# Layer B of a two-layer encoder: three units of two head pairs by one level of Strassen's products, its normalisation applied to x, and a reordered first microsecond

## The chip, the core and the metric

The kernel runs on one core of a Trainium2 chip. The metric is the device time of one execution in microseconds (us). The profile's rows name PE (matrix products), PEld (its weight loads), DVE (vector engine), ACT (scalar engine), POOL (GpSimd) and SP, which issues most DMAs.

## What is computed

Two layers over 512 tokens of width 1024, one batch. Layer A mixes tokens by dilated window attention (three dilation groups), layer B by neighbourhood attention on an 8 x 64 grid. Both have 16 heads of 64 columns, which the kernel handles as 8 pairs (`hc` 0 to 7).

```python
hn = rms_norm(x, norm_gain[i])
proj = hn @ w_in
q, k, v, gate = jnp.split(proj, 4, axis=-1)      # layer B
q = rms_norm(q, q_gain) * HEAD_DIM ** -0.5
k = rms_norm(k, k_gain)
...
p = jax.nn.softmax(logits)
y = (p @ v) * jax.nn.silu(gate)
x = x + y @ w_out
```

In layer B a pair takes 384 columns of q, k and v and 128 gate columns; the depth of each product is 1024.

## The kernel before, in words

All values are float32. Every matrix product is made from three of the reduced type: an operand is rounded by ACT (`_h`), the remainder is taken by a subtraction on DVE or POOL (`_l`), and `mm3` (L330) issues h x h, h x l and l x h into one PSUM bank. The activations stand in `hn_h` and `hn_l` (k = 0 to 7 slices of 128 x 512), the weights stream through 8 raw buffers (`wraw`), are rounded to `wh` (6 buffers) and split to `wl` (5 buffers).

`Plan` (L180) lists the weight blocks ("jobs") in the order of use, each 384 or 512 columns wide, and decides when the load of each is issued (`lead`, L269: 4, 12 or 6 jobs ahead) and whether POOL or DVE takes the remainder (`pool`, L296). `mixed` (L217) is the plan of a Strassen unit: four blocks of weights, two of which are added in place by DMAs that POOL issues with an accumulate (`add`, L209), and one sum on DVE (`sum`, L203). Only layer A has such units before.

PE's order is written by hand. `run` (L1163) lets a main generator emit the projections and a side generator emit the attention in between, by a clock that counts PE's work (`clock`, `stamp`, `later_on`). The other engines' order is the scheduler's, except where `in_order` or `keep_in_program_order` holds it.

In layer A, `main_a` (L692) makes the k, v, q columns of a pair by seven half-size products: `product` (L360) multiplies 4 slices of depth for two token tiles, and its evacuations combine the results (`put_v`, `put_u`, `put12`, `put22`, `put21`). The mixed left operands are made once by `mix` (L531) from x already multiplied by its norm factors (`scale_x`, L518).

In layer B, `main_b` (L1259) projects each pair plainly: `project_qk` (L622) takes 8 slices of depth for four token tiles, ACT multiplies the result by the row's norm factor on the way out of PSUM, POOL squares q and k, and `project_t` (L401) makes the gate, which DVE multiplies by half the norm factor (`rs_half`). `side_b` (L1275) is the attention of a pair: transposes of q and k, `scores`, `softmax` (DVE minimum, ACT exponential, ACT scaling), then the turn of the probabilities: by DVE transposes and a round trip through DRAM (`turner`, L914) for pairs 0 to 5, by PE transposes (`turn_p`, L1351) for pairs 6 and 7, then `weigh` and `put_y`. `out_product` (L1197) is the output projection; it starts on the pairs that are done.

At the start, `load_x` brings x in four loads between the weights' loads, the gains come by two small loads of ACT's queue, nine products of ones run on PE while it waits, and `square_a` (L510) squares each slice of x on ACT with a running sum on POOL.

Of the kernel before, what the change touches and what calls it, by code (L numbers as in the profile page):

```python
# [22 lines left out]
P = 128  # L23
# [4 lines left out]
KT = 8  # L28
# [7 lines left out]
PB = 4  # L36

# [9 lines left out]
def tile_hybrid_encoder(  # L47
# [5 lines left out]
    norm_gain: bass.AP,  # L53
    head_gain: bass.AP,
# [80 lines left out]
    mix_h = big.tile([P, 4, 4, H], F32R, tag="yh", name="mix_h")  # L135
    mix_l = big.tile([P, 4, 4, H], F32R, tag="yl", name="mix_l")
# [19 lines left out]

    def cast(raw, n):
        h = wp.tile([P, 512], F32R, tag="wh", name="wh", bufs=6)[:, :n]
        act.copy(h, raw)
        return h, raw, n  # L160
# [19 lines left out]
    class Plan:  # L180
# [22 lines left out]
        def sum(self, at, dst, a, b, eng):  # L203

            for raw in (dst, a, b):
                raw.used(at)
            self.sums.setdefault(at, []).append(lambda: eng.tensor_add(home(dst), a.tile, b.tile))

        def add(self, at, dst, off):  # L209

            dst.used(at)
            src = lambda: w[:, off : off + dst.cols]
            self.sums.setdefault(at, []).append(
                lambda: pol.dma_start(dst.tile, src(), accum_op=ALU.add)
            )

        def mixed(self, hc):  # L217
            b, j = hc * A_HC, len(self.jobs)
            b11, b21, b12, b22 = ([self.raw(b + 2048 * n + 1024 * i) for i in range(2)] for n in range(4))
            gate = self.raw(b - A_HC + 1152 * KT)  # L220
            v = self.raw(b - A_HC + 1024 * KT)
            t2 = [self.raw(None) for _ in range(2)]
            late = hc == 1
            order = (b11, gate, b21, b11, t2, b22, b12, v, t2) if late else (b11, gate, b21, v, b11, t2, b22, b12, t2)
            for part in order:
                for raw in part if isinstance(part, list) else [part]:
                    self.use(raw, 128 if raw in (gate, v) else 512)
# [23 lines left out]
    for hc in range(1, NHC):  # L251
        plan.mixed(hc)
# [11 lines left out]
    for hc in range(NHC):  # L264
        plan.plain(B_IN + hc * B_HC, 384, KT)
        plan.plain(B_IN + hc * B_HC + 384 * KT, 128, KT)
    outs(B_OUT)

    def lead(raw):  # L269
        return 4 if raw.first < start_jobs else 12 if raw.first < mixed_jobs else 6  # L270
# [46 lines left out]
    stamp = {("qk", -1): 0, ("w", -1): 0}  # L317
    stamp |= {("yb", -i, "y"): 0 for i in (1, 2, 3)}
# [41 lines left out]
    def product(acc, stat, open_, evac, guard=None):  # L360
# [4 lines left out]
        for k in range(KH):  # L365
# [4 lines left out]
            for i in range(2):  # L370
                sh, sl = (t[:, P * i : P * i + P] for t in stat(k))
                mm3(acc[i], sh, sl, h, l, open_ and k == 0, k == KH - 1, skip_group_check=True)
                if k == KH - 1:
                    evac(i, acc[i])
                yield

    def project(stat_h, stat_l, n, evac, guard, need=None, after=None):
# [3 lines left out]
        for k0 in range(0, KT, both):  # L381
# [6 lines left out]
            ws = [next(wsteps) for _ in ks]  # L388
            for i in range(4):
# [7 lines left out]
            if after:  # L397
                yield "xn", k0
                after(k0)
# [26 lines left out]
    later = []  # L426

    def head_norm(raw, ss, ns, late):
# [10 lines left out]
        if late:  # L439
            later.append(lambda: [tc.keep_in_program_order(scale(i)) for i in range(4)])  # L440
            return
# [17 lines left out]
    ng = cp.tile([P, 2, KT], F32, name="ng")  # L459
# [13 lines left out]
    pq = wk.tile([P, 4096], F32, tag="pt", name="pt", bufs=1)  # L473
    x_all = pq.rearrange("p (k t) -> p k t", k=KT)

    def load_x(k0, k1):
        syn.dma_start(x_all[:, k0:k1, :], xt[:, k0:k1, :])
# [5 lines left out]
    act.dma_start(ng, norm_gain)  # L483
# [6 lines left out]
    for _ in range(9):  # L490
# [4 lines left out]
    hg = cp.tile([P, 8], F32, name="hg")  # L495
    act.dma_start(hg, head_gain)
# [13 lines left out]
    def square_a(k):  # L510
# [3 lines left out]
        act.activation(sq, x_all[:, k, :], AF.Square)  # L514
# [3 lines left out]
    def scale_x():  # L518

        pa = spread()  # L520
        for k in range(KT):
            xk = x_all[:, k, :]
            vec.scalar_tensor_tensor(xk, xk, ng[:, 0, k : k + 1], pa, op0=ALU.mult, op1=ALU.mult)
            stamp["xn", k] = 0
# [6 lines left out]
    def mix():  # L531

# [3 lines left out]
        a, b = t[:, 0], t[:, 1]  # L536

        def put(n, out, op, x, y, eng, wait=0):
            def split():
                with in_order():  # L540
                    eng.tensor_sub(mix_l[:, n], out, mix_h[:, n].bitcast(F32))
                stamp["mix", n] = 0
# [5 lines left out]

        yield "wait", ("first",), 500
# [53 lines left out]
    rk = wk.tile([P, 4096], F32, tag="rawk", name="rawk", bufs=1)  # L603
# [5 lines left out]
    def raw_b(hc, cols):  # L609
        if hc % 3 < 2:  # L610
            return part(hc % 3, cols)
        if "third" not in st:
            st["third"] = wk.tile([P, 2048], F32, tag="rawq", name="rawb", bufs=1)
        return st["third"][:, : 4 * cols].rearrange("p (i c) -> p i c", i=4)

    def raw_q():
        return wk.tile([P, 4, 512], F32, tag="rawq", name="rawq", bufs=1)
# [4 lines left out]
    def project_qk(n, ns, key, hc, guard, first=False, **kw):  # L622
# [3 lines left out]
        def evac(i, acc):  # L626
            if not box:
                box.append(raw_q() if key == "rawq" else part(0) if key == "rawk" else raw_b(hc, n))
# [19 lines left out]
    def normed(raw, ss, ns, key, hc):  # L648

        def go():  # L650
            with in_order() if hc == 0 and key != "raw" else nullcontext():
                head_norm(raw, ss, ns, key == "raw")
# [39 lines left out]
    def main_a(hc):  # L692
        if hc == 0:
            yield from project_qk(512, 8, "rawq", hc, None, first=True, need="na")
            yield from project_qk(512, 4, "rawk", hc, ("rs", "a"), after=renorm)
# [10 lines left out]
        mixed = lambda n: lambda k: (t[:, n, k, :] for t in (mix_h, mix_l))  # L706
# [36 lines left out]
        for n, acc, first, put in ((0, c, True, put_v), (1, b, True, put_u), (3, c, False, put12), (2, b, False, put22)):  # L743
            yield "mix", n
# [103 lines left out]
    def put_y(hc, o, last):  # L848
# [4 lines left out]
        h, l = st["y_h"][:, hc, :], st["y_l"][:, hc, :]  # L853
        for grid, line in ((mid_rc, mid_o), (edge_rc, edge_o)):
            vec.tensor_mul(grid(gt), grid(gt), line(o))
        act.copy(h, gt)
        (vec if last else pol).tensor_sub(l, gt, h.bitcast(F32))
        stamp["yb", hc, "y"] = 0

# [9 lines left out]
    def y_back(hcs, tag):  # L869
        t = wk.tile([P, 4 * S], F32, tag=tag, name="yr", bufs=1)  # L870
        y = t[:, : len(hcs) * S].rearrange("p (n s) -> p n s", n=len(hcs))
        syn.dma_start(y, y_d[:, hcs[0] : hcs[-1] + 1, :])
        return t, y
# [40 lines left out]
    class turner:  # L914
# [12 lines left out]
        def send(self, dst, wait, pace, key=None):  # L927
# [8 lines left out]
            def read(b):  # L936
# [3 lines left out]
                if key and not self.left:  # L940
# [6 lines left out]
    def attn_a(hc):  # L947
# [202 lines left out]
        st["tail"], back = y_back(range(2), "tr")  # L1150
# [391 lines left out]
```

## Time and profile before

| what | us |
|---|---|
| median of 3 runs (lowest to highest) | 837.17 (836.69 to 837.88) |
| the profiled execution | 836.45 |
| its span on the core | 834.7 |
| layer A's pairs, about | 83 to 540 |
| its output product, about | 540 to 578 |
| layer B's pairs, about | 578 to 791 |
| last weighting and output product, about | 803 to 835 |

Times inside a profile count from the start of the span. The lines of each view are quoted in the prediction.

### The profile page before, as it was taken

Reading aid. Unit: us, or ns where it says so; the run is one execution under the profiler, and the core shown is the slowest. Engines: PE = TensorE matmul, PEld = TensorE weight load, DVE = VectorE, ACT = ScalarE, POOL = GpSimd, SP = SyncE. Lnnn points to the kernel's source line nnn. Section 1 sums busy time; section 2 is a strip of 40 time slices with the busy share of each in tenths; the row PEclk is TensorE's granted clock in tenths of the full one; section 3 lists DMA queues with packets and bytes.
Section 4 is the critical chain, followed back from the end, with each engine's and each line's share of the span. In section 5 each row is a group of like instructions: output and inputs, shape, how many; then the busy total and the mean of one; then the engine's idle time right before and its main releaser. Section 6 shows DMA issues by size and latency. Waiting matters only on the chain.

```text
span 834.7 us, 18138 instructions
## 1 busy us (share of the span) xinstructions
PE 821.2 (98%) x6611; PEld 685.0 (82%) x6611; DVE 631.2 (76%) x1653; ACT 506.6 (61%) x1066; POOL 292.9 (35%) x259
## 2 busy tenths in 40 slices
PE   8999999999999999999999999999999999999998
PEld 6877878878877878878878877789998899989786
DVE  7899897897897787786787866657578777876742
ACT  7657766846846846846846837645366654666440
POOL 5032442553543543543443424312133222333201
PEclk9999999999999999999999999999999999999999
DMA  9426756576686775775776664283254466544212
GB/s 340 149 57 164 195 148 160 120 177 206 121 183 203 164 170 174 164 175 169 161 170 180 137 195 158 75 296 111 93 186 153 126 170 190 165 143 138 86 51 102
DMA packets 56169, 131.97 MB, mean 158 GB/s; under 512 B 7184, under 2 KB 24528, under 8 KB 55952
## 3 DMA queue, kind: packets, MB, share of 16 engines
q1 hardware_dynamic: 49456, 108.39, 41.7%
q0 software_dynamic: 6048, 22.02, 15.2%
q8 instruction: 52, 0.85, 0.4%
q10 hardware_dynamic: 576, 0.41, 0.2%
q14 instruction: 37, 0.30, 0.1%
HBM read 111.73 MB, written 11.72 MB: 148 GB/s over the span
## 4 chain that ended last, share of the span: by engine, by line
PE 87%; DVE 4%; ACT 4%; DMA 3%; issue 1%; SPq 0%; DVEq 0%; ACTq 0%
PE acc L324 72%; PE log L324 5%; PE o L324 5%; PE tp L328 4%; DVE wl L85 1%; DMA wraw<-in_w 1%; DMA yr<-y_d 1%; DVE rawq L85 1%; ACT wh L85 1%; DMA pt<-in_xt 1%; ACT p L85 0%; ACT rawk L85 0%; DVE ss L85 0%; DVE mixed L85 0%; ACT sq L85 0%
## 5 line engine op out<-in xcount | busy, mean ns | idle before, releaser
L85 POOL TENSOR_TENSOR wl<-wraw,wh 128x512 fp32r<-128x512 f32 (+1 forms) x153 | 199.2, 1303 | 401.1 <-PE acc L324 161.4
L85 ACT CAST wh<-wraw 128x512 fp32r<-128x512 f32 (+1 forms) x360 | 208.5, 593 | 180.6 <-PE acc L324 137.1
L85 DVE TENSOR_TENSOR wl<-wraw,wh 128x512 fp32r<-128x512 f32 (+1 forms) x207 | 161.5, 783 | 39.0 <-PE acc L324 22.6
L324 PE MATMUL acc<-wh,hn_h 128*128 128x384 f32 (+1 forms) x488 | 184.4, 378 | 1.2 <-DVE rawq L85 1.2
L324 PE MATMUL acc<-wl,hn_h 128*128 128x384 f32 (+1 forms) x488 | 176.9, 362 | 2.9 <-DVE wl L85 2.9
L324 PE MATMUL acc<-wh,hn_l 128*128 128x384 f32 (+1 forms) x488 | 176.6, 362 | 0.0
L85 ACT ACTIVATE p<-p,mn 128x256 f32<-128x256 f32 (+2 forms) x248 | 138.2, 583 | 23.2 <-DVE mn L85 23.2
L324 PEld LDWEIGHTS acc<-wh,hn_h 128*128 128x128 f32 x488 | 91.7, 188 | 17.0 <-issue 6.8
L324 PEld LDWEIGHTS acc<-wl,hn_h 128*128 128x128 f32 x488 | 91.8, 188 | 11.9 <-DVE wl L85 4.7
L324 PEld LDWEIGHTS acc<-wh,hn_l 128*128 128x128 f32 x488 | 91.6, 188 | 9.6
L324 PE MATMUL acc<-wh,mix_h 128*128 128x512 f32 x224 | 89.0, 397 | 0.0
L324 PE MATMUL acc<-wh,mix_l 128*128 128x512 f32 x224 | 87.4, 390 | 0.0
L324 PE MATMUL acc<-wl,mix_h 128*128 128x512 f32 x224 | 87.3, 390 | 0.0
L324 PE MATMUL acc<-hn_h,wh 128*128 128x512 f32 x192 | 78.2, 407 | 0.0
L324 PE MATMUL acc<-hn_h,wl 128*128 128x512 f32 x192 | 75.3, 392 | 0.0
L324 PE MATMUL acc<-hn_l,wh 128*128 128x512 f32 x192 | 74.9, 390 | 0.0
L85 DVE STREAM_TRANSPOSE pt<-p 128x512 f32<-128x512 f32 (+1 forms) x60 | 40.6, 687 | 23.6 <-ACT p L85 23.4
L324 PE MATMUL acc<-y_h,wh 128*128 128x512 f32 x128 | 51.7, 404 | 0.5 <-ACT gt L85 0.5
L85 DVE TENSOR_REDUCE ss<-sq 128x4 f32<-128x256 f32 (+1 forms) x96 | 45.7, 498 | 8.1 <-ACT sq L85 4.3
L324 PEld LDWEIGHTS acc<-wh,mix_h 128*128 128x128 f32 x224 | 42.0, 188 | 9.8 <-issue 1.6
L324 PE MATMUL acc<-y_h,wl 128*128 128x512 f32 x128 | 50.0, 391 | 0.0
L324 PE MATMUL acc<-y_l,wh 128*128 128x512 f32 x128 | 49.9, 390 | 0.0
(148 smaller groups left out, 1358.5 us busy)
## 6 DMA issues: line engine op xcount, KB each, us to landing
wraw<-in_w SPq DMA_DIRECT2D x95, 512.0 KB
wraw<-in_w POOLq DMA_DIRECT2D x42, 512.0 KB, 7.0
wraw<-in_w SPq DMA_DIRECT2D x38, 384.0 KB
pt<-pt SPq DMA_DIRECT2D x106, 64.0 KB
td<-tr SPq DMA_DIRECT2D x24, 224.0 KB
pt<-td SPq DMA_DIRECT2D x24, 224.0 KB
e<-l_d SPq DMA_DIRECT2D x32, 112.0 KB
e<-l_d SPq DMA_DIRECT2D x16, 128.0 KB
```

Source lines behind the costliest of these rows:

```text
L85: m = f(*args, **kw)
L324: nc.tensor.matmul(o, l, r, **kw)
L328: nc.tensor.transpose(o, i, ident)
```

## The change

One: layer B. Pairs 0 and 1 keep the plain projection, without their gates. Pairs 2 to 7 become three units of two pairs, `unit_b`, each with seven products of 4 slices, two token tiles and 384 columns; the gates of the two pairs of the unit before are made inside the unit, those of 6 and 7 after the last. While pair 1 is projected, `scale_x(1)` multiplies x by the norm factors, `renorm` rounds it again into `hn_h` and `hn_l`, and `mix_b` makes the mixed operands. In the units the evacuations combine like layer A's, and the squares are ACT's. The outputs of pairs 0 to 3 go to DRAM (`y_d`) and come back in one load of 1 MB while the last unit ends. Pairs 6 and 7 are turned on PE after the last unit.

Two: the start. The gains stand in front of x in one array and come with its first slice. The squares stand behind the rounding of the next weights. The first step of the first projection issues h x h for all four token tiles, then h x l, then l x h. Eight products of ones instead of nine.

Also: one buffer of 6144 columns holds what were `rawk`, `rawq` and `rawb`, and `lead` and `pool` have entries for the units.

```diff
+        m = act.copy(h, raw)
+        if len(rounded) <= KT:
+            rounded.append(m.ins)
...
+        with tc.issue_after(rounded[k + 1]):
+            act.activation(sq, x_all[:, k, :], AF.Square)
...
-    for _ in range(9):
+    for _ in range(8):
...
+            if need and not k0:
+                h, l = ws[0]
+                for n_, (s, m) in enumerate(((stat_h, h), (stat_h, l), (stat_l, h))):
+                    for i in range(4):
+                        matmul(acc[i][:, :n], s(0, i), m, start=n_ == 0, stop=False)
+                        yield
+                continue
...
+    for hc in range(2, NHC, 2):
+        plan.mixed(in_b(hc + 1), in_b(hc), 384, gate_w(hc - 2), gate_w(hc - 1))
...
-            pool[0] = [0, 1] if first < 16 else [1, 2] if at < mixed_jobs else [2, 5]
+            pool[0] = [0, 1] if first < 16 else [1, 2] if at < mixed_jobs else [3, 5] if units_at <= at < units_end else [2, 5]
...
+    def mix_b():
+
+        put, a, b, x11, x12, x21, x22 = mixer(1)
+        put(0, a, vec.tensor_sub, x21, x22, pol)
...
-    def main_b(hc):
-        yield from project_qk(384, 4, "raw", hc, ("qk", hc - 1) if hc else ("rs", "b"))
-        acc = []
-        yield from project_t(acc)
...
-        tc.keep_in_program_order(vec.tensor_mul(gt, acc[0], st["rs_half"]))
...
+    def unit_b(r):
+
+        l = r + 1
...
+        def put11(i, acc):
+            act.copy(left[:, i, :], acc)
+            squares(left[:, i, :256], sl, i, 4)
+
+        def put_v(i, acc):
+            vec.tensor_sub(right[:, 2 + i, :], acc, left[:, 2 + i, :])
...
+        def put22(i, acc):
+            t = right[:, 2 + i, :]
+            vec.tensor_sub(t, t, acc)
+            squares(t[:, :256], sr, 2 + i, 4)
...
+        part_of = partial(product, cols=384)
+        yield from part_of(a, hn(0, 0), True, keep, ("w", r - 4))
+        yield from gate_a(r - 2)
+        yield from part_of(a, hn(KH, 0), False, put11)
+        yield from gate_a(r - 1)
+        yield "mix", 1, 0
+        yield from part_of(c, mixed(0), True, put_v, ("w", r - 3))
+        for n, acc, first, put in ((1, b, True, put_u), (3, c, False, put12), (2, b, False, put22)):
+            yield "mix", 1, n
+            yield from part_of(acc, mixed(n), first, put)
+        normed(right, sr, 4, "raw", r)
...
+        yield from part_of(b, hn(KH, H), False, put21)
+        normed(left, sl, 4, "raw", l)
+
+    def main_b():
...
+        yield from project_qk(384, 4, "raw", 0, ("rs", "b"))
+        yield from project_qk(384, 4, "raw", 1, None, after=(1, renorm))
+        stamp["renormed",] = 0
+        for r in range(2, NHC, 2):
+            yield from unit_b(r)
+        for hc in range(NHC - 2, NHC):
+            yield from gate_a(hc)
...
+            if hc == NHC - 4:
+                yield "wait", ("yb", "back"), 0
+                back = y_back(range(NHC - 4), wk.tile([P, 2048], F32, tag="tr", name="yr", bufs=1))
+                later_on(1000, partial(y_put, hc))
+                for n in range(NHC - 4):
+                    later_on(8000 + 2000 * n, partial(y_put, n, back[:, n, :]))
+                yield from side_b(hc + 2)
```

Three places show how the instructions move.

ACT at the very start, before. `pt` is x, `ng` the gains, `ssq` and `sqx` are the squares, `wh` the rounded weights.

```order
L85 ACTIVATE hn_h_92<-pt_98,ng_96 128x512
L85 ACTIVATE ssq_169<-pt_98 128x512
L85 CAST wh_125<-wraw_114 128x512
L85 ACTIVATE hn_h_92<-pt_98,ng_96 128x512
L85 ACTIVATE sqx_179<-pt_98 128x512
L85 CAST wh_127<-wraw_114 128x512
L85 ACTIVATE hn_h_92<-pt_98,ng_96 128x512 x2
```

The same place after the change:

```order
L84 ACTIVATE hn_h_92<-pt_95 128x512
L84 CAST wh_120<-wraw_109 128x512
L84 ACTIVATE hn_h_92<-pt_95 128x512
L84 CAST wh_122<-wraw_109 128x512
L84 ACTIVATE ssq_162<-pt_95 128x512
L84 ACTIVATE hn_h_92<-pt_95 128x512 x2
```

The first two roundings of weights now stand ahead of all squares.

PE in the projection of a middle pair, before: one weight block (`wh_8624`, `wl_8632`) serves four token tiles, that is twelve products, of which the last six are these.

```order
L324 MATMUL acc_8765<-wh_8624,hn_h_92 128x384
L324 MATMUL acc_8765<-wl_8632,hn_h_92 128x384
L324 MATMUL acc_8765<-wh_8624,hn_l_93 128x384
...
L324 MATMUL acc_8766<-wh_8624,hn_h_92 128x384
L324 MATMUL acc_8766<-wl_8632,hn_h_92 128x384
L324 MATMUL acc_8766<-wh_8624,hn_l_93 128x384
```

After the change, at the end of a unit's last mixed product (operands `mix_`) and the start of its last plain one:

```order
L332 MATMUL acc_8738<-wh_8814,mix_h_7376 128x384
L332 MATMUL acc_8738<-wl_8830,mix_h_7376 128x384
L332 MATMUL acc_8738<-wh_8814,mix_l_7377 128x384
L332 MATMUL acc_8739<-wh_8814,mix_h_7376 128x384
L332 MATMUL acc_8739<-wl_8830,mix_h_7376 128x384
L332 MATMUL acc_8739<-wh_8814,mix_l_7377 128x384
L332 MATMUL acc_8738<-wh_8828,hn_h_92 128x384
L332 MATMUL acc_8738<-wl_8849,hn_h_92 128x384
L332 MATMUL acc_8738<-wh_8828,hn_l_93 128x384
```

A weight block now serves two token tiles, six products; and bank `acc_8738`, which `put22` has to read after the mixed product, is written again by the product right behind it.

DVE at that same point of the unit, after the change (`rawk_153` is the buffer in which the results are combined):

```order
L84 TENSOR_TENSOR wl_8891<-wraw_8508,wh_8876 128x384
L84 TENSOR_TENSOR rawk_153<-rawk_153,acc_8738 128x384
L84 TENSOR_TENSOR wl_8937<-wraw_8712,wh_8899 128x384
L84 TENSOR_TENSOR rawk_153<-rawk_153,acc_8739 128x384
L84 TENSOR_REDUCE ss_8275<-sq_8907 128x4
```

The two subtractions into `rawk_153` are `put22` for the unit's two token tiles; a weight remainder stands between them. In layer B DVE had no such combinations before.

More of the change, by code (lines that the diff above doesn't have):

```diff
@@ L36 @@
 PB = 4
+G = 24
 A_HC = 1280 * KT
@@ L213, in add, with mixed @@
             self.sums.setdefault(at, []).append(
-                lambda: pol.dma_start(dst.tile, src(), accum_op=ALU.add)
+                lambda: pol.dma_start(dst.tile[:, : dst.cols], src(), accum_op=ALU.add)
             )
[L217 to L223, printed above, removed]
+        def mixed(self, left, right, n, gate, v, late=False):
+            j, c = len(self.jobs), 2 * n
+            b11, b21, b12, b22 = ([self.raw(b + c * (k + i), c) for i in range(2)]
+                                  for b in (left, right) for k in (0, 2))
+            gate, v = self.raw(gate), self.raw(v)
+            t2 = [self.raw(None, c) for _ in range(2)]
             order = (b11, gate, b21, b11, t2, b22, b12, v, t2) if late else (b11, gate, b21, v, b11, t2, b22, b12, t2)
@@ L607, in part, with raw_b @@
         return half.rearrange("p (i c) -> p i c", i=4)
[L609 to L614, printed above, removed]
+    def raw_b(hc):
+        at = 1536 * (0, 1, 3, 2, 1, 0, 2, 3)[hc]
+        return rk[:, at : at + 1536].rearrange("p (i c) -> p i c", i=4)
     def raw_q():
-        return wk.tile([P, 4, 512], F32, tag="rawq", name="rawq", bufs=1)
+        return rk[:, 4096:].rearrange("p (i c) -> p i c", i=4)
     def sums():
@@ L1155, in attn_a @@
         yield from q_a(hc + 1)
-        _, more = y_back(range(2, NHC - 2), "rawq")
+        more = y_back(range(2, NHC - 2), rk[:, 4096:])
         for n in range(2, NHC - 2):
@@ L1273, in tile_hybrid_encoder @@
+    def main_b():
+        for key in ("gate", "pt", "w"):
+            for hc in range(NHC):
+                stamp.pop((key, hc), None)
+        yield from project_qk(384, 4, "raw", 0, ("rs", "b"))
[3 more added lines that the diff above has]
+            yield from unit_b(r)
+        for hc in range(NHC - 2, NHC):
+            yield from gate_a(hc)
     far = lambda hc: hc < NHC - 2
     def side_b(hc):
[L1276 to L1279 removed]
@@ L1359, in weigh @@
         def weigh():
-            assert not any(t.left for t in turners)
             o = bank("o")
@@ L1407, in main @@
             st["e", hc] = bias_b(hc)
-        for hc in range(NHC):
-            yield from main_b(hc)
+        yield from main_b()
         yield from out_product("yb", sink_b)
@@ L1423, in side @@
         stamp["rs", "a"] = 0
-        for _ in scale_x():
+        for _ in scale_x(0):
             pass
@@ L1441, in side @@
         stamp["rs", "b"] = 0
-        yield 5000
-        st["rs_half"] = wk.tile([P, 2, S], F32, tag="q12", name="rs_half", bufs=1)[:, 0]
-        act.mul(st["rs_half"], spread(), 0.5)
-        stamp["rs", "all"] = 0
-        for hc in range(NHC):
-            yield from side_b(hc)
+        yield 3000
+        for _ in scale_x(1):
+            pass
+        yield 2000
+        yield from mix_b()
+        for hc in range(0, NHC - 2, 2):
+            yield from side_b(hc)
+            yield from side_b(hc + 1)
+            yield from weigh_b(hc)
+            if hc == NHC - 4:
[5 more added lines that the diff above has]
+                yield from side_b(hc + 2)
+            yield from weigh_b(hc + 1)
+            if hc == NHC - 4:
+                y_put(hc + 1)
+        hc = NHC - 2
+        yield from st.pop(("turn", hc))()
+        yield from side_b(hc + 1)
+        put_y(hc, st.pop(("weigh", hc))(), False)
+        yield 1000
+        yield from st.pop(("turn", hc + 1))()
+        stamp["yb", "turned"] = 0
+        put_y(hc + 1, st.pop(("weigh", hc + 1))(), True)
+        yield
         yield from residual(xm_d)
```

190 lines of the change are left out of this document (109 added, 81 removed).

## The prediction

> **What bounds the kernel now.** I read the page first: busy shares, then the chain that ended last, then the granted clock.
>
> ```profile
> span 834.7 us, 18138 instructions
> PE 821.2 (98%) x6611; PEld 685.0 (82%) x6611; DVE 631.2 (76%) x1653; ACT 506.6 (61%) x1066; POOL 292.9 (35%) x259
> PEclk9999999999999999999999999999999999999999
> PE 87%; DVE 4%; ACT 4%; DMA 3%; issue 1%; SPq 0%; DVEq 0%; ACTq 0%
> ```
>
> PE is busy 98% of the span, at full clock, and is 87% of the chain. Such a busy time can hide slack between pipelined products, so I next look at the pace of products in layer B, by their starts.
>
> ```profile
> 616.13 0.33 PE L324 MATMUL acc<-wl,hn_h 128*128 128x384 f32 x1
> ...
> 622.03 0.34 PE L324 MATMUL acc<-wh,hn_l 128*128 128x384 f32 x1
> ```
>
> These are two of 35 consecutive products of 384 columns: 34 intervals in 5.90 us, 0.1735 us each, although each row shows 0.33 us. Nothing lies between them: in layer B's projections PE issues without pause. The last view of this part is the busy time by stage (columns: window; its length, then PE, PEld, DVE, ACT, POOL busy with counts; clock; DMA share; GB/s).
>
> ```profile
> 140.00:202.00 62.00, 61.81 (x590) 49.89 (x588) 50.66 (x125) 39.65 (x79) 27.38 (x22) 1.00 0.68 170
> 681.10:734.70 53.60, 53.60 (x355) 49.19 (x354) 40.14 (x131) 32.21 (x86) 16.07 (x18) 1.00 0.56 167
> 37.00:43.00 6.00, 6.00 (x28) 4.97 (x27) 6.00 (x11) 3.64 (x7) 1.30 (x1) 1.00 0.28 87
> ```
>
> The first is one Strassen unit of layer A, the second two pairs of layer B. Both are PE's, and layer A shows that seven products with their sums can be fed: DVE 82%, ACT 64%, POOL 44%. The third shows DVE full for 6 us with PE losing nothing, since weights are prepared some jobs ahead.
>
> **The change part by part.** The sum is made against the profiled execution, 836.45 us (834.7 of span and 1.75 around it); the median of the runs, 837.17, is 0.7 above it.
>
> *Products removed.* A plain pair takes 8 slices x 4 tiles x 3 = 96 products of 384 columns, two pairs 192. A unit takes 7 x 4 x 2 x 3 = 168. Three units save 72, at 0.1735 us: **-12.5 us**. The gates, scores, transposes and weightings are the same in number. This is on the path wherever PE is.
>
> The Trainium skill, "TensorE: Matmul & The Clock Gate", section "Wait — 56ns, not 53.3ns?", gives N divided by 2.4 GHz plus about 2.5 ns for a warm product, 162.5 ns for 384 columns. By it the saving would be 11.7 us; the trace's 173.5 ns differ, and the measurement decides.
>
> *The start.*
>
> ```profile
> 3.87 0.72 ACT L85 ACTIVATE hn_h<-pt,ng 128x512 fp32r<-128x512 f32 x1 [0.70 <-DMA ng<-in_norm_gain]
> 4.50 0.62 ACT L85 ACTIVATE ssq<-pt 128x512 f32<-128x512 f32 x1
> 5.09 0.62 ACT L85 CAST wh<-wraw 128x512 fp32r<-128x512 f32 x1
> 5.76 0.80 PE L324 MATMUL acc<-wh,hn_h 128*128 128x512 f32 x1
> 6.95 0.50 PE L324 MATMUL acc<-wl,hn_h 128*128 128x512 f32 x1 [0.39 <-DVE wl L85]
> 19.68 0.50 PE L324 MATMUL acc<-wl,hn_h 128*128 128x512 f32 x1 [1.03 <-DVE wl L85]
> 14.44 3.49 DVE L85 SCALAR_TENSOR_TENSOR hn_l<-pt,ng,hn_h 128x512 fp32r<-128x512 f32 x2
> 21.25 1.40 DVE L85 SCALAR_TENSOR_TENSOR hn_l<-pt,ng,hn_h 128x512 fp32r<-128x512 f32 x2
> 14.27 3.12 POOL L85 TENSOR_TENSOR ssq<-ssq,sqx 128x512 f32<-128x512 f32 x2 [0.30 <-ACT sqx L85]
> ```
>
> ACT waits 0.70 us for the gains and squares for 0.62 us before it rounds the first weights: without both, the first product starts up to 1.2 us earlier; the eight products of ones probably hold it to about 0.7. Then PE stands from 5.76 to 6.95 for `wl`; three more h x h products fit there, about 0.9 us. So PE may be 1.6 us ahead after the first step. But it stands again before 19.68, because DVE takes 3.49 us for a pair of remainders while POOL adds squares, against 1.40 us when POOL is done. DVE then sets the pace, and those additions remain. Ends: -2.3 (all of it, and half of the later stall) and 0 (DVE gives nothing). I take **-1.1**. The two gain loads vanish from ACT's queue; x's first slice grows by 24 columns.
>
> *Elementwise work in a unit.* Means by form; the first seven from 628.5 to 734.7 (four pairs), the rest from layer A, 327 to 389.
>
> ```profile
> L85 ACT CAST wh<-wraw 128x384 fp32r<-128x384 f32 x31 | 15.6, 509 | 14.3 <-PE acc L324 14.3
> L85 DVE TENSOR_TENSOR wl<-wraw,wh 128x384 fp32r<-128x384 f32 x16 | 9.3, 579 | 0.0
> L85 POOL TENSOR_TENSOR wl<-wraw,wh 128x384 fp32r<-128x384 f32 x16 | 17.2, 1075 | 50.5 <-PE acc L324 31.9 <-issue 10.6 <-ACT wh L85 4.9
> L85 POOL TENSOR_TENSOR sq<-rawk 128x256 f32<-128x256 f32 x8 | 4.9, 616 | 7.8 <-ACT rawk L85 5.9 <-DVE mn L85 1.9
> L85 ACT ACTIVATE rawk<-acc,rs_n 128x384 f32<-128x384 f32 x8 | 4.5, 561 | 0.0
> L85 DVE TENSOR_TENSOR ql<-tp,qh 128x384 fp32r<-128x384 f32 x4 | 2.2, 558 | 5.6 <-ACT qh L85 5.6
> L85 DVE TENSOR_TENSOR gt<-acc,rs_half 128x512 f32<-128x512 f32 x4 | 2.7, 684 | 0.0
> L85 ACT ACTIVATE sq<-rawk 128x256 f32<-128x256 f32 x4 | 1.7, 414 | 0.4 <-DVE rawk L85 0.4
> L85 ACT COPY rawk<-acc 128x512 f32<-128x512 f32 x4 | 2.4, 588 | 0.2
> L85 POOL DMA_DIRECT2D wraw<-in_w x6 | 5.3, 876 | 1.2 <-POOL wl L85 0.6 <-PE acc L324 0.3 <-DVE rawq L85 0.3
> L85 DVE TENSOR_TENSOR wraw<-wraw 128x1024 f32<-128x1024 f32 x2 | 2.5, 1226 | 4.3 <-DMA wraw<-in_w 3.1 <-POOL wl L85 1.2
> ```
>
> A unit replaces two pairs, and PE's 53.6 us become 53.6 - 24 x 0.1735 = 49.4. DVE gains ten combinations at about 0.56 (the 384-column row that also reads PSUM) and two weight sums of 768 columns at 1.226 x 3/4, and loses two products with `rs_half`; its remainders stay nearly the same in number, since three of five go to POOL: +5.6 +1.8 -1.4 -0.1 = +5.9, that is 46.0 of 49.4 us, 93%. ACT: 12 more roundings (+6.1), eight scaled evacuations less (-4.5), four plain copies of 384 columns (+1.8, the 512 row scaled), eight squares (+3.3), two gate halvings at the copy's row (+1.2): 40.1, 81%. POOL: about seven more remainders of 384 (+7.9), two of 512 (+2.9, the 384 row scaled), no squares (-4.9), six issues of adding DMAs (+5.3): 27.3, 55%. All this lies beside PE as long as each `wl` comes in time; if that cover goes, every us of DVE beyond 49.4 is a us of time. On average nothing is lost. The mixing (`scale_x`, `mix_b`, a second rounding of x) lies beside the 192 products of pairs 0 and 1, 33 us, where no gates are made.
>
> *Bursts.* A softmax fills ACT for some 10 us, and PE needs a rounding each 6 x 0.1735 = 1.04 us in a unit, where before it was each 2.08. PE has up to five jobs in hand, 5.2 us. Six bursts fall into the units; each may cost nothing, when the list has the roundings in time, or about 1.2. Nothing below zero: no list can be faster than PE's. I take **+3.0** (0 to +7).
>
> *A bank written again at once.*
>
> ```profile
> 171.54 0.39 PE L324 MATMUL acc<-wh,mix_l 128*128 128x512 f32 x1
> 172.12 0.47 PE L324 MATMUL acc<-wh,hn_h 128*128 128x512 f32 x1 [0.19 <-DVE rawq L85]
> 171.28 1.37 DVE L85 TENSOR_TENSOR rawq<-rawq,acc 128x512 f32<-128x512 f32 x2 [1.06 <-PE acc L324]
> ```
>
> In layer A, PE goes from the last mixed product to `put21`'s product in 0.58 us instead of 0.23, as `put22` must first read the bank. Units of layer B have the same place. There three products of 0.17 cover the first reading instead of three of 0.23, so about 0.4; the weight remainder that stands between the two readings adds up to 0.4. Three units: **+1.8** (1.1 to 2.4). Queued behind the waiting product is all of PE.
>
> *The end.*
>
> ```profile
> 771.33 0.44 PE L328 MATMUL tp<-ident,p 128*128 128x128 f32 x2 [0.26 <-ACT p L85]
> 772.61 0.33 PE L328 MATMUL tp<-ident,p 128*128 128x128 f32 x1 [0.84 <-ACT p L85]
> 494.16 8.41 DMA yr<-y_d
> ```
>
> PE waits 1.1 us for pair 6's softmax; after the change a gate, a weighting and output products stand between scores and turn: **-1.1** (or 0). Against it, 1 MB of outputs comes back, and in ACT's list its four roundings stand ahead of pair 6's q. Layer A's return of half that size took 8.4 us. SP issues it behind pair 5's round trip. If late, ACT, then pair 6's scores, then PE wait: 0 to +3; I take **+1.0**. The 256 KB stores of four outputs wait on nothing that PE needs.
>
> Sum: -12.5 -1.1 +3.0 +1.8 -1.1 +1.0 = -8.9, so 827.6 beside 836.45; with the profile a little under the median, I say **828.0**.
>
> **The rivals.** *No list loses anything* (chance 0.15): without the bursts and the return 823.6, with all of the start 822.4; the 82% to 100% of DVE that PE bore above speak for it.
>
> *DVE becomes the bound of the units* (0.20): 93% is a mean, and the pairs of rows at 14.44 and 21.25 show two-operand DVE work at 2.5 times its time beside POOL's. POOL goes from 30% to 55% in a unit. If a tenth is added to DVE's 46.0, it needs 50.6 against 49.4, and waits in its list add one or two more: +1 to +3.5 a unit instead of the 1.0 in the sum, some +4 to +7 in all: 832 to 835. It decides once DVE's busy time in a unit passes PE's. Against it speaks layer A's unit with POOL at 44%. The Trainium skill, "SBUF — State Buffer", section "Who interferes with whom", calls the pair of ports that DVE and GpSimd share an exclusive lock. The trace agrees where the two engines meet (3.49 against 1.40 us).
>
> *The additions land late* (0.07), the case that ends slower.
>
> ```profile
> DMA to landing us min/median/max: 5.2/7.0/10.7
> ```
>
> Each unit adds two blocks in place nine jobs before they are used again; with four in hand, 13 x 1.04 = 13.5 us, less POOL's queue (0.9 and two remainders, 3.0 together), a rounding and a remainder (1.6): 8.9 us. Layer A has a job each 1.36 us and so some 4 us more. Above 8.9 us each us costs ACT, then PE, twice a unit, six in all. At the median's 7.0 it costs nothing; at 11.2 us, 13.8: 841. The share of DMA time, 0.56 before, grows by 18 additions, which speaks for it; blocks a quarter smaller speak against it.
>
> **How the numbers follow.** Forecast, 824 to 831: 0.55. Stall-free, 821 to 824: 0.15. DVE-bound: 0.20, a fifth of it above 835.5. Late additions: 0.07. That gains and losses cancel for a reason not seen: 0.03. The range 821.0 to 835.5 holds about 0.87 of these; its ends come from the sum's bounds, -14.8 and -0.1 (-12.5 +3 +2.4 +7), the upper cut where fewer than one in ten lie. A measurement here tells 0.2%, 1.7 us, from no change. Faster than that: 0.55 + 0.15 + 0.16 = 0.86. Same: 0.06. Slower: 0.08.
>
> **What would show it.** PE's list 72 products shorter and a unit of about 50 us between equal scores confirm the first term. The first real product near 5.0 us and no stall behind it confirm the start. A stall of 0.4 to 0.8 us where a bank is written again, three times, confirms that term. DVE at 97% or more of a unit with PE waiting for `wl` or `rawk` shows the second rival; ACT idle for a DMA into `wraw` followed by PE's wait shows the third. The forecast is wrong if PE idles more than 8 us between 580 and 790.

## The result and the profile after

The changed kernel takes 890.52 us (median of 4 runs, 888.17 to 892.08) beside 837.52 us before: the ratio is 1.0627, with an interval of 1.0602 to 1.0653. The forecast was 828.0, and the change costs 53 us. The page's first lines of the changed kernel:

```profile
span 889.4 us, 18293 instructions
PE 832.6 (94%) x6538; PEld 688.0 (77%) x6538; DVE 688.2 (77%) x1703; ACT 536.1 (60%) x1133; POOL 347.3 (39%) x291
PEclk9999999999999999999999999997899989899999
```

PE's list is 73 instructions shorter, as the forecast counted (72 products and one of ones). Yet PE is busy longer, and the granted clock, full in every slice before, drops by the page's digits in four of the 40 slices, from the 28th (600 us) on. The windows that answer to the first two of before:

```profile
140.00:202.00 62.00, 61.36 (x586) 49.58 (x585) 50.76 (x126) 39.65 (x79) 27.15 (x21) 1.00 0.71 170
681.10:734.70 53.60, 46.02 (x270) 40.50 (x269) 44.14 (x123) 33.17 (x93) 20.07 (x19) 0.94 0.65 175
```

Layer A is as before. In layer B PE idles 7.6 of 53.6 us, and DVE, at 82%, is no fuller than in layer A, where PE is busy 61.4 of 62 us. Next the waits of PE behind 578 us, before (one row) and after (the largest; columns: what waited, for whom, total us, times, longest):

```profile
PE tp L328 <- ACT p L85: 1.1, 2, 0.8
```

```profile
PE log L332 <- DVE kl L84: 11.8, 5, 6.0
PE tp L336 <- DVE rawk L84: 11.5, 3, 6.2
PE acc L332 <- DVE wl L84: 7.6, 3, 3.5
PE o L332 <- DMA td<-tr: 3.9, 1, 3.9
PE log L332 <- DVE gt L84: 2.6, 1, 2.6
PE log L332 <- DVE ss L84: 2.1, 1, 2.1
```

Most of it is DVE's: q and k of a pair (`rawk`, `kl`) that PE must turn and score, and weight remainders (`wl`). Then come the turned probabilities, on their way through DRAM. In sum PE idled 34 us from 578 to 790 us, where the forecast called itself wrong above 8. The windows of layer B, the first two lines of before, the others of after:

```profile
578.00:600.00 22.00, 22.00 (x127) 20.93 (x128) 12.45 (x41) 8.58 (x17) 6.59 (x8) 1.00 0.24 78
600.00:640.00 40.00, 40.00 (x263) 36.67 (x261) 28.64 (x103) 27.12 (x77) 11.37 (x14) 1.00 0.47 147
```

```profile
578.00:600.00 22.00, 19.31 (x116) 18.75 (x114) 19.10 (x43) 10.27 (x20) 11.91 (x12) 0.98 0.28 84
600.00:640.00 40.00, 26.88 (x130) 23.69 (x131) 34.45 (x76) 23.47 (x54) 18.91 (x16) 0.75 0.33 83
640.00:690.00 50.00, 44.57 (x278) 39.60 (x278) 39.61 (x100) 28.23 (x70) 22.10 (x23) 0.97 0.74 187
690.00:740.00 50.00, 42.78 (x250) 38.05 (x247) 39.68 (x105) 30.91 (x89) 20.13 (x21) 0.93 0.72 196
740.00:790.00 50.00, 44.21 (x258) 39.68 (x257) 39.73 (x120) 32.27 (x91) 19.82 (x21) 0.90 0.58 140
```

From 578 to 640 us DVE is busy 53.6 of 62 us (41.1 before), and PE 46.2. In the units DVE is at 79%, POOL at 41%, and PE loses 5 to 7 us in each 50. Two mechanisms can be read in the timeline. **DVE is held by POOL.** These are DVE's and POOL's rows in two places:

```profile
742.06 0.55 DVE L84 TENSOR_TENSOR rawk<-rawk,acc 128x384 f32<-128x384 f32 x1
742.53 3.68 DVE L84 SCALAR_TENSOR_TENSOR na<-na,nv 128x16 f32<-128x16 f32 x1
746.24 0.18 DVE L84 SCALAR_TENSOR_TENSOR rs<-na,rs 128x16 f32<-128x16 f32 x1
```

```profile
742.05 0.86 POOL L84 DMA_DIRECT2D wraw<-in_w  x1 [1.30 <-DVE rawk L84]
742.62 3.54 POOL L84 TENSOR_TENSOR wl<-wraw,wh 128x512 fp32r<-128x512 f32 x3
```

```profile
719.48 3.28 DVE L84 TENSOR_TENSOR wl<-wraw,wh 128x384 fp32r<-128x384 f32 x1
723.02 0.55 DVE L84 TENSOR_TENSOR wl<-wraw,wh 128x384 fp32r<-128x384 f32 x1
```

```profile
719.15 3.19 POOL L84 TENSOR_TENSOR wl<-wraw,wh 128x384 fp32r<-128x384 f32 x3
```

An operation on 16 columns, 0.18 us elsewhere, takes 3.68 us and ends when POOL's third remainder in a row ends; a remainder of 0.55 us takes 3.28 in the same way. From 578 to 810 us, DVE's rows that exceed their usual time (the median of the same operation) by over 0.7 us all stand beside POOL's operations: there are 8 such rows with 6.8 us too much before, and 24 with 37.4 us after. This excess is called held time below.

**A stall slows what follows.** These are PE's rows behind the stall at 597 us, and two windows with the granted clock (the third number from the end):

```profile
600.97 1.48 PE L336 MATMUL tp<-ident,rawk 128*128 128x128 f32 x4 [3.66 <-DVE rawk L84]
602.56 0.52 PE L332 MATMUL acc<-wl,hn_h 128*128 128x384 f32 x1
602.88 0.52 PE L332 MATMUL acc<-wh,hn_l 128*128 128x384 f32 x1
```

```profile
602.00:606.00 4.00, 4.00 (x14) 4.00 (x14) 2.94 (x4) 1.65 (x3) 0.00 (x0) 0.50 0.01 4
597.00:845.00 248.00, 204.66 (x1186) 177.58 (x1185) 195.38 (x516) 143.28 (x371) 99.28 (x92) 0.91 0.57 150
```

After 3.66 us of idling, products of 384 columns start each 0.32 us instead of 0.1735, until 606 us. The granted clock is 0.50 there, and 0.91 on average from 597 to 845 us; the trace has only full and half clock, so this is half clock for some 45 us. At seven of the eight stalls above 2.5 us such a stretch begins within 5 us of the stall's start; the kernel before has none between 578 and 830 us. Between consecutive products of the projections, delays of under 0.5 us beyond the pace add up to 18 us (4 in the same part of the kernel before), beside 43 us of stalls. So the stalls bring a second loss with them, by this count an estimated 14 us.

### The profile page after: what moved, and what is told of

It reads as the page before. It is cut to its first block, busy times and chain, and to the rows that moved or that the text cites. A ratio compares the mean times of both kernels' runs of the same rounds, so it can differ in the third digit from the quotient of the medians.

```text
span 889.4 us, 18293 instructions
## 1 busy us (share of the span) xinstructions
PE 832.6 (94%) x6538; PEld 688.0 (77%) x6538; DVE 688.2 (77%) x1703; ACT 536.1 (60%) x1133; POOL 347.3 (39%) x291
## 3 DMA queue, kind: packets, MB, share of 16 engines
q1 hardware_dynamic: 50176, 110.50, 39.7%
## 5 line engine op out<-in xcount | busy, mean ns | idle before, releaser
L84 POOL TENSOR_TENSOR wl<-wraw,wh 128x512 fp32r<-128x512 f32 (+1 forms) x185 | 238.3, 1304 | 407.7 <-PE acc L332 170.1
L332 PE MATMUL acc<-wh,hn_h 128*128 128x512 f32 (+1 forms) x368 | 145.2, 396 | 2.6 <-DVE rawk L84 1.9
L332 PE MATMUL acc<-wl,hn_h 128*128 128x512 f32 (+1 forms) x368 | 138.5, 378 | 1.7 <-DVE wl L84 1.7
L332 PE MATMUL acc<-wh,hn_l 128*128 128x512 f32 (+1 forms) x368 | 137.8, 376 | 0.0
L332 PE MATMUL acc<-wl,mix_h 128*128 128x512 f32 (+1 forms) x320 | 122.1, 382 | 7.7 <-DVE wl L84 7.6
L332 PE MATMUL acc<-wh,mix_h 128*128 128x512 f32 (+1 forms) x320 | 123.6, 386 | 0.0
L332 PE MATMUL acc<-wh,mix_l 128*128 128x512 f32 (+1 forms) x320 | 121.3, 379 | 0.0
L332 PEld LDWEIGHTS acc<-wl,mix_h 128*128 128x128 f32 x320 | 61.8, 193 | 17.8 <-DVE wl L84 9.0
L84 POOL DMA_DIRECT2D wraw<-in_w x60 | 52.8, 890 | 47.1 <-PE acc L332 11.0
L332 PEld LDWEIGHTS acc<-wh,mix_l 128*128 128x128 f32 x320 | 61.8, 193 | 8.9
L84 DVE STREAM_TRANSPOSE pt<-p 128x512 f32<-128x512 f32 (+1 forms) x60 | 40.6, 687 | 23.7 <-ACT p L84 23.6
```

The lines of the kernel that those rows point to most:

```text
L84: m = f(*args, **kw)
L332: nc.tensor.matmul(o, l, r, **kw)
```

## The experiments

Times are medians; the kernel before stood between 836.9 and 838.0 in every set of runs. Each kernel differs from the changed one (890.5) by its edit, unless another is named. Edits 3, 7, 12, 13 and 14 leave out work that a right result needs; they tell only what that work costs. The profiles reach layer B at 562.9 to 568.9 us although the edits lie behind that place; so a place is named by the times of its own profile, and a difference of 2 us between two medians says little.

**1. Transposes and scores of pair 0 and 1 later in PE's list (`p_later`).**

```diff
-        yield "wait", ("raw", hc), 9000 if hc < 2 else ...
+        yield "wait", ("raw", hc), 16000 if hc < 2 else ...
-        yield 1750 if hc < NHC - 1 else 1250
+        yield 7000 if hc < 1 else 1750 if hc < NHC - 1 else 1250
```

> PE's hand-written order is changed alone: the transposes of pair 0's and 1's q and k stand about 5 us of PE work later, pair 0's scores 10 us later. Theory 'lists and the lock' (PE stands behind a transpose or a score product whose DVE work is queued behind the mixing, and DVE is held while POOL runs remainders back to back): the stalls of 3.8, 6.2 and 6.3 us at 597, 610 and 627 us shrink to under a third of their 16.4 us and the slow products behind them go too, 872 to 880 us against the 890.5 of the changed kernel. Rival 'DVE has too much work' : the stalls only move, 886 to 893. Rival 'the adding DMAs land late': nothing changes, 888 to 893.

It takes 887.98 us. The stalls moved: they are 1.5, 1.3 and 3.4 us at 604, 610 and 614 us, 6.6 at 630, and 5.3 at 693 and 7.1 at 733 in place of smaller ones. With the mixing in DVE's list, a later place of these products in PE's list is worth little.

**2. No remainders on POOL in the units (`u_pool0`).**

```diff
-            ... else [3, 5] if units_at <= at < units_end else [2, 5]
+            ... else [0, 1] if units_at <= at < units_end else [2, 5]
```

> All weight remainders of the three units go to DVE instead of three in five to POOL. Theory 'lists and the lock': the long rows of DVE (2.8 and 3.3 us for a remainder that takes 0.55) disappear from the units, DVE's busy time there does not grow by more than 3 us a unit although it gets some 20 remainders more, and the time falls to 872 to 884. Rival 'DVE has too much work': 20 remainders of 0.55 a unit, three units, some 33 us more work on the engine that bounds, 900 to 925. Rival 'the adding DMAs land late': POOL issues them sooner, at most 5 us less, 885 to 891.

It takes 882.85 us, 7.7 less. DVE's busy time did not grow over the whole kernel (685.9 us beside 688.2), though it has 57 instructions more, some 19 remainders a unit. These windows answer to the first two of the units above (39.61 and 39.68 for DVE); in the third, 740 to 790 us, DVE is busy 43.0 us beside 39.7:

```profile
640.00:690.00 50.00, 43.06 (x256) 37.92 (x258) 38.16 (x116) 25.88 (x64) 4.28 (x5) 0.93 0.74 185
690.00:740.00 50.00, 42.95 (x253) 38.27 (x250) 39.03 (x126) 32.55 (x92) 4.32 (x5) 0.93 0.77 200
```

So POOL's share bought nothing: what it took over it took from DVE again by holding it. But PE loses as much as before (it is busy 43 of 50 us), waiting at other places.

**3. The adding loads left out (`u_noadd`).** `Plan.mixed` issues its three `add` only for layer A.

> The 18 loads that are added in place to weight blocks of layer B are left out, so that layer B multiplies by blocks that are not summed; all products stay. Rival 'the adding DMAs land late': the stalls in the units go, 868 to 880. Theory 'lists and the lock': only the issuing on POOL goes (18 of 0.9 us), remainders bunch less, 884 to 891. Rival 'DVE has too much work': 888 to 893.

It takes 875.98 us, 14.5 less: more than any theory but the rival's had said. In the changed kernel ACT never waited for a block to land, though; the page gives the adding loads 4.9 us from issue to landing, where the forecast allowed 8.9. What the adding loads do is in the changed kernel's groups by form, 640 to 800 us (busy and mean, then idle time of POOL ahead of them and who ended it):

```profile
L84 POOL DMA_DIRECT2D wraw<-in_w x14 | 12.4, 886 | 25.5 <-DVE na L84 7.6 <-PE log L332 7.0 <-DMA wraw<-in_w 4.6
L84 DVE TENSOR_TENSOR wl<-wraw,wh 128x384 fp32r<-128x384 f32 x30 | 23.1, 771 | 7.4 <-ACT wh L84 3.5 <-issue 3.0 <-ACT sq L84 0.4
```

POOL stands 25.5 us in front of 14 issues and takes 0.89 us for each; the remainders queued behind them then run back to back, and DVE's mean remainder is 771 ns beside 579 in the kernel before and 640 in this run.

**4. Edits 1 and 2 together (`both`).**

> The edits of the later transposes and of no remainders on POOL in the units together. Theory 'lists and the lock': the two gains add, 856 to 870. Rival 'DVE has too much work': 895 or more. Rival 'the adding DMAs land late': 885 to 891.

It takes 882.26 us: nothing beyond edit 2.

**5. No units (`zero_units`, `zero_units2`).** Pairs 2 to 7 are plain, from the x that is rounded again, each followed by the gate of two pairs before; no mixing.

```diff
-        for r in range(2, NHC, 2):
-            yield from unit_b(r)
+        for hc in range(2, NHC):
...
+            yield from project_qk(384, 4, "raw", hc, ("w", hc - 4))
+            yield from gate_a(hc - 2)
```

> No Strassen units: pairs 2 to 7 are projected plainly from the x that is rounded again, and nothing is mixed; start, gains, second rounding, gates and the way of four outputs by DRAM stay as in the changed kernel. If units and mixing hold the loss: 836 to 845 (before is 837 to 838; the second rounding may cost the 3.8 us of the first stall). If the second rounding and the new end hold it: 855 or more.

It takes 850.84 us. In this form all pairs wrote one place of the buffer, which also overwrites results still in use; the second form has four places.

> The run without units again, with each pair's results in the buffer place of the pair four before it (in the earlier one all pairs shared a single place, so that each waited for the one before it). No units, no mixing; start, gains, second rounding, gates and the way of four outputs by DRAM stay. If units and mixing hold the loss: 836 to 845. If the second rounding and the new end hold it: 850 or more.

It takes 848.72 us: 11 us slower than before without any unit, so some of the loss is not the units'. Its profile shows two stalls. One is the 3.5 us of the first transposes. The other is this, ACT's and SP's rows and PE's largest wait:

```profile
764.25 2.17 ACT L84 CAST y_h<-yr 128x512 fp32r<-128x512 f32 x4 [9.20 <-DMA yr<-y_d]
```

```profile
755.10 0.32 SPq L84 DMA_DIRECT2D yr<-y_d  x1
```

```profile
PE acc L335 <- ACT rawk L84: 6.3, 2, 6.1
```

ACT stands 9.2 us for the 1 MB that SP issued at 755.1, and pair 7's copies out of PSUM stand behind it.

**6. Two units (`two_units`).** Pairs 2 and 3 plain, units for 4 to 7.

> Pairs 2 and 3 are projected plainly from the x that is rounded again, so two units stay and the mixing has 33 us of plain products more beside it; 24 products of 384 columns more (4.2 us). If each unit loses for itself, as much as its stalls (about 12 us with the slow products behind them): 880 to 884. If the crowding of the mixing into pair 1 and the first unit is what costs most: 862 to 872.

It takes 891.24 us: neither. There is only one stall of 0.6 us beside the plain pairs, from 636 to 690 us, but 10.1 us of stalls remain from 597 to 636 (15.8 in the changed kernel), and in the two units and the end PE stalls for 30 us, 10.5 of them at once at 797 us, for normalised q and k. So the loss is not so much a unit. Giving the mixing a neighbour with slack helps little; it still stands in DVE's list ahead of pair 0's q and k.

**7. No remainders of the units' weights (`u_norest`).** `queue.append((h, h, m))` in place of `rest`.

> The remainders of the units' weights are left out: PE multiplies by the rounded weights in their place, all products stay (layer B is then less exact). DVE and POOL lose together 54 subtractions a unit. Theory 'DVE's list' (DVE is late because of the amount in its list and of POOL's holding it): stalls from 636 to 800 us fall from 28 to under 10 and the time to 858 to 870. Rival 'latency' (transposes, scores and turns stand too early in PE's order whatever the load): 878 to 890.

It takes 871.59 us, 18.9 less, near the first theory's range. Its stalls are not as that theory said, though: from 636 to 800 us they stay (21.9 us beside 21.8), and those ahead of 636 us fall from 15.8 to 6.8. In the units DVE falls to between 27.8 and 34.6 of 50 us, and yet PE waits, most of all for the round trips:

```profile
PE o L332 <- DMA pt<-td: 12.2, 3, 5.4
PE log L332 <- DVE kl L84: 7.4, 4, 4.9
```

**8. Mixing, second rounding and squares off POOL too (`pool0_mix`, on top of edit 2).** `pol` becomes `vec` in `mix_b` and `renorm`, and `squares` go to ACT.

> As the run without POOL's remainders in the units, and also the mixed operands' remainders, those of the second rounding and the squares of pairs 0 and 1 are taken from POOL (to DVE, the squares to ACT). Theory 'POOL holds DVE': the 5.1 us row of DVE at the mixing becomes 1.2, and although DVE gets 5.1 us more work, the time falls to 874 to 879 against 882.9. Rival 'DVE has too much work': 884 to 890.

It takes 883.20 us beside 882.85: no difference. That the work which DVE gains and the holding which it loses cancel here is a reading; no run parts them.

**9. Weightings of pairs 0 and 2 later (`o_later`, on top of edit 8).** `weigh_b` waits 9000 instead of 4000 for these two.

> Against the run with POOL's remainders, mixing and squares taken away (883.2): the weightings of pairs 0 and 2 stand 5.3 us of PE work later in PE's list, and nothing else moves. Theory 'the turns come late' (PE stands before a weighting until the probabilities are back from DRAM): the two stalls of 5.3 and 4.3 us go and the slow products behind them, 870 to 875. Rival 'DVE is the bound behind them': the time appears at the next wait for DVE, 880 to 884.

It takes 885.49 us: neither gain nor, quite, the rival's case. Of pair 0's stall 0.7 us is left, but PE waits 6.9 us at 669 and 6.5 us at 738 for the probabilities of pairs 1 and 3. Their weightings stand where they stood, and waited 0.9 us and less there. So the round trips of both pairs are late.

**10. Outputs' remainders on DVE (`y_vec`, on top of edit 8).** `vec` instead of `pol` in `y_put`.

> Against the same run (883.2): the remainders of the outputs (y_l) go from POOL to DVE, five 512-column subtractions. Theory 'POOL holds DVE': the 16-column operations of 1.2 us at 801 to 806 take 0.17 again, the stall of 4.3 us at pair 7's scores goes: 878 to 880. Rival 'DVE has too much work': 883 to 887.

It takes 878.65 us, 4.5 less than edit 8 (875.9 to 882.3). Of the 4.0 us stall at pair 7's scores under 0.5 is left. This is the fastest of those with three units that leave nothing out.

**11. The kernel before, with three in five remainders of layer B on POOL (`b_pool35`).** One number in its pool table.

> The kernel before, with three in five weight remainders of layer B on POOL instead of two in five; PE's list stays the same. Theory 'POOL holds DVE': DVE's rows beside POOL's get longer, about as much as DVE has less to do, and PE, which had 25 per cent of slack there, loses 0 to 4 us: 837 to 841. Rival 'DVE's amount of work': DVE gets less to do and the time stays, 836 to 838, with DVE's busy time in 640 to 790 us lower by 8 us or more.

It takes 837.72 us, ratio 0.9997 (0.9983 to 1.0011). DVE's held time rises from 6.8 to 12.4 us, its busy time in 640 to 790 us falls by 3.3 us only (112.4 to 109.1), and PE waits no longer than before. Here the holding alone costs nothing.

**12. Plain loads and small adding loads (`u_plainadd`, `u_smalladd`).** Same places in POOL's list; in the first, whole blocks are overwritten, in the second 96 of 768 columns are added.

> The 18 adding loads of layer B become plain loads of the same size, at the same places of POOL's list, that write over the block instead of adding to it (so the blocks are not sums). If what the adding loads cost is POOL standing before each issue and for 0.9 us: nothing changes, 887 to 892. If it is the work of adding in the DMA engines: 876 to 881, as with the loads left out (876.0).

It takes 889.27 us: adding is no dearer than copying.

> The 18 adding loads of layer B add 96 of their 768 columns only (the rest of the block is not a sum): same places in POOL's list, same waits, an eighth of the bytes. If an adding load costs what POOL stands and issues: 886 to 891. If it costs the bytes on the DMA engines (busy 0.73 to 0.76 of the time in the units): 876 to 880, as with the loads left out (876.0).

It takes 883.34 us (878.3 to 884.9): between the two. About half of the 14.5 us goes with the bytes and half with POOL's standing and issuing; the spread leaves the share open.

**13. No mixing (`u_nomix`).** Mixed operands are replaced by slices of x; `mix_b` is gone.

> Nothing is mixed in layer B: the products of mixed operands take slices of the rounded x instead; all products, sums of weights and combinations of results stay. If mixing crowded into pair 1 and the first unit holds the loss of 578 to 640 us (stalls of 13.5 and slow products of 2.5 after 597): 872 to 877. If other work behind it keeps DVE as full: 884 to 890.

It takes 878.37 us, 12.1 less. From 578 to 640 us PE idles 7.2 us instead of 15.8.

**14. Edits 3, 7 and 13 together (`u_none`).**

> Mixing, the adding loads and the remainders of the units' weights are all left out together (as in the three runs that leave out one each); all products stay. If these three crowd the lists and are the loss of the units, only what the kernel without units loses is left, 848.7 - 12.5 = 836, and the time is 834 to 844. If the places of turns, scores and weightings in PE's list lose by themselves: 852 to 862.

It takes 850.49 us, 40.0 less, where the three alone gave 45.6 in sum. What is left, 14 us above 836, is more than the first theory had and less than the second. Its waits:

```profile
PE log L334 <- ACT kh L84: 4.1, 2, 2.8
PE log L334 <- DVE kl L84: 3.9, 3, 3.2
PE tp L338 <- DVE rawk L84: 2.7, 1, 2.7
PE o L334 <- DMA pt<-td: 2.3, 3, 1.2
```

**15. Returned outputs later in ACT's list (`z_ylate`, on the second form of edit 5).**

```diff
+                yield from side_b(hc + 2)
                 for n in range(NHC - 4):
-                    later_on(8000 + 2000 * n, partial(y_put, n, back[:, n, :]))
-                yield from side_b(hc + 2)
+                    with tc.issue_after(st["exp"]):
+                        y_put(n, back[:, n, :])
```

> The kernel without units (848.7), and the four roundings of outputs that come back from DRAM stand behind pair 6's last exponential in ACT's list instead of ahead of its q. If ACT's wait of 9.2 us for them is what stops PE for 6.2 us at 761: 840 to 843. If PE then waits for something else there: 846 to 849.

It takes 841.76 us, 7.0 less; no stall above 0.5 us is left behind the one at 597 us.

**16. And pair 0's transposes later (`z_tplate`, on edit 15).** Its wait is 16000.

> The kernel without units and with the later roundings of outputs (841.8), and the transposes of pair 0 stand 8 us of PE work later. The stall of 3.6 us at 597, where they wait for normalised results behind the second rounding in DVE's list, has other products ahead of it then. If a place in PE's list is worth something once DVE is not full behind it (without mixing): 836 to 839. If the stall only moves, as it did with the mixing in place: 841 to 844.

It takes 836.02 us, ratio to before 0.9987 (0.9971 to 1.0003). This is the same kind of edit as the first, and without the mixing it works. DVE is about as full as in the changed kernel (53.6 of these 62 us), but PE runs on:

```profile
578.00:640.00 62.00, 60.12 (x377) 57.52 (x377) 54.48 (x166) 38.40 (x100) 23.58 (x25) 1.00 0.46 143
```

No kernel tried beats the one before by more than a measurement can tell.

## Why the prediction was wrong

The loss adds up from the runs:

| what | us |
|---|---|
| without units, return and first transposes in better places (edit 16) | 836.0 |
| the transposes' place (edit 16 against 15) | +5.7 |
| the return (edit 15 against 5) | +7.0 |
| products removed (the forecast's term) | -12.5 |
| mixing, adding loads and remainders (edit 14) | +40.0 |
| the rest, found by difference | +14.3 |

Together this is 890.5, and each piece but the -12.5, which is the forecast's own, and the rest is a difference of two runs. Two cautions belong to it. That return and transposes cost as much beside units as without them is assumed, and for the return it does not fit: in the changed kernel ACT stood 1.76 us for it, not 9.2 (row below), so part of the 7.0 belongs to other pieces. And edit 14 leaves out all 84 weight remainders of the units, while six plain pairs need 48; so the 40.0 is likely more than the units add, and the rest likely more than 14.3.

*Products removed.* The count and the pace were right: the list is shorter, and an undisturbed product still starts each 0.1735 us. It brought no gain because PE was not left to set the pace.

*The mixing and the second rounding* is the step that failed first. The forecast let them lie "beside the 192 products of pairs 0 and 1, 33 us". But x is scaled only when its row factors are known, and what DVE does from then on stands in one list ahead of pair 0's q and k. Four of DVE's rows show it, in the changed kernel:

```profile
584.40 3.36 DVE L84 SCALAR_TENSOR_TENSOR pt<-pt,pa 128x512 f32<-128x512 f32 x5
...
600.49 1.42 DVE L84 TENSOR_TENSOR rawk<-rawk,rs 128x256 f32<-128x256 f32 x4
```

```profile
610.40 5.08 DVE L84 TENSOR_TENSOR mix_l<-mixed,mix_h 128x1024 fp32r<-128x1024 f32 x1
615.40 0.74 DVE L84 SCALAR_TENSOR_TENSOR kl<-tp,gk,kh 128x512 fp32r<-128x512 f32 x1
```

Pair 0's normalised q and k come at 600.5, and its scores wait 6.0 us for a `kl` of 0.74 that stands behind a mixed remainder of 5.08 (1.2 us when POOL is quiet). So this term, put at nothing, has a price: edit 13 shows 12.1 us for the mixing, and edit 16 shows 5.7 us for the place of the transposes.

*Elementwise work in a unit.* The forecast expected 46.0 of 49.4 us on DVE and concluded that on average nothing is lost. DVE was busy less, 79%, and PE waited all the same. Edit 2, in which DVE has more to do and the kernel is faster, shows that the amount alone does not decide. The step that failed is the inference from the average, and with it the row for a remainder, 579 ns, which was 771 in the units. The bursts, +3.0 with a bound of 7, were mis-sized: by the rows at 742 us, what fills a list is not a softmax alone but POOL's issue, three remainders behind it and what DVE has queued meanwhile. The forecast also had no term for the clock, which a stall lowers for what follows.

*The rivals.* "DVE becomes the bound" named the place and the holding by POOL, but priced the first at 4 to 7 us and let it decide once DVE's busy time passes PE's. PE lost time to DVE far below that. "The additions land late" had the right object, worth 14.5 us, and the wrong mechanism: the blocks landed in time. POOL stood at the issues, and about half of the price went with the bytes, by a way that no run shows. The Trainium skill, "SBUF — State Buffer", section "Who interferes with whom", says that a DVE instruction with two inputs in SBUF, as these have, contends with a GpSimd instruction that reads SBUF; for DVE's two-port mode it says that whoever comes first keeps the shared pair for the whole instruction and the other blocks fully. The rows at 742 and 719 us agree that DVE is held and go further: it did not get its turn between POOL's instructions, but stood for three of them.

*The bank written again at once* was forecast at +1.8 (1.1 to 2.4), and this term held. The first of the three places:

```profile
672.45 0.34 PE L332 MATMUL acc<-wh,mix_l 128*128 128x384 f32 x1
673.00 0.41 PE L332 MATMUL acc<-wh,hn_h 128*128 128x384 f32 x1 [0.21 <-DVE rawk L84]
...
673.43 0.34 PE L332 MATMUL acc<-wh,hn_l 128*128 128x384 f32 x1
673.84 0.44 PE L332 MATMUL acc<-wh,hn_h 128*128 128x384 f32 x1
674.12 0.34 PE L332 MATMUL acc<-wl,hn_h 128*128 128x384 f32 x1
```

From 672.45 to 674.12 there are five starts where five times 0.1735 would be 0.87 us: 0.80 us too much, first for the reading of one bank, then for that of the other, behind the weight remainder. The second place costs 0.80 us as well. At the third, DVE's two readings stand next to each other, and it costs 0.56. In all this is 2.2 us.

*The start*, -1.1, gave nothing that can be measured: layer B's first product starts at 566.0 us, at 565.2 before. ACT's and PE's rows:

```profile
5.15 0.62 ACT L84 CAST wh<-wraw 128x512 fp32r<-128x512 f32 x1 [0.82 <-DMA wraw<-in_w]
```

```profile
5.82 1.19 PE L332 MATMUL acc<-wh,hn_h 128*128 128x512 f32 x4 [0.58 <-ACT wh L84]
23.74 0.50 PE L332 MATMUL acc<-wl,hn_h 128*128 128x512 f32 x1 [1.05 <-DVE wl L84]
```

ACT was free sooner, but then it waited for the first weights until 5.15, where before it rounded them at 5.09. The reordered first step works (four products without a stall), and a later wait for `wl`, at 23.7, takes it back, as the forecast's end of 0 had it.

*The end.* Pair 6's stall went, as forecast. The return was given +1.0 with a bound of 3, argued from a load of half the size that took 8.4 us. Without units ACT stood 9.2 us for it, and edit 15 shows a price of 7.0 us: what stood behind it in ACT's list were pair 7's copies, not pair 6's q. In the changed kernel ACT has other work until 808.2 us, and stands for less:

```profile
809.92 2.18 ACT L84 CAST y_h<-yr 128x512 fp32r<-128x512 f32 x4 [1.76 <-DMA yr<-y_d]
```

What the return costs there no run shows.

What stays open is the rest of 14.3 us, whose waits are spread over scores, turns and weightings; the split of an adding load's cost between bytes and POOL's list; and how much of each piece is the clock's.

## What to carry to other kernels

A mean share of 80% on a helper engine was no cover here: what counts is what stands ahead of the one result that PE needs next, in each in-order list, and how long the longest uninterrupted stretch of it is. Work that is needed once and soon (a mixing, a second rounding) belongs in such a sum of one list and one deadline, not in an average over a stage. And PE can pay for a stall twice, as the products behind it may run at half clock. Moving an instruction in PE's list helps only if what it waits for is not merely late by the same amount again.

## What the runs showed of the hardware

A DVE instruction of 0.18 us was held for 3.68 us while POOL ran three subtractions in a row. In b_pool35 the held time was 12.4 us, with no loss of time. After a stall of 3.66 us PE ran products of 384 columns at 0.32 us instead of 0.1735 for 4 us, at a granted clock of 0.50; from 600 to 640 us, with three stalls, the clock was 0.75 on average. And an adding load cost no more than a plain one of the same size (889.3 and 890.5 us).
